# Scores of two heads in the two halves of the array, transposes as two of 64 rows, and a new order of the attention steps

## The chip, the cores and the metric

The kernel runs on one core of one Trainium2 chip. The metric is the device time of one execution in microseconds, the median of several runs. TensorE is called PE below, its weight loads PEld, VectorE DVE, ScalarE ACT, GpSimd POOL, and SyncE, which issues the large transfers, SP.

## What is computed

Two layers of a hybrid decoder over 512 tokens of width 1024. In each layer one projection makes q, k, v and a gate for 16 heads of width 64: 8 "dilated" heads, whose mask is the mixture of three dilated windows, and 8 "forgetting" heads, whose scores get a cumulative log of a forget gate as a bias. In between stands the norm of q and k, then causal softmax attention, the SiLU gate, the output projection and a gated embedding.

```python
qa = rms_norm(heads(qa), qk_g[0]); ka = rms_norm(heads(ka), qk_g[1])
s = einsum('bqhd,bkhd->bhqk', q_i, k) * scale          # forgetting heads
s = s + c_i[..., :, None] - c[:, :, None, :]           # c = cumsum(log_f)
prob = softmax(where(causal, s, NEG)); o = prob @ v
...
ob = dilated_attention(qb, kb, vb)                      # three (window, dilation) pairs
h = h + concatenate([oa * silu(ga), ob * silu(gb)]) @ w_out
gate = sigmoid(rms_norm(h, ple_norm_g) @ w_ple_gate)
h = h + (p_i @ w_ple) * gate
```

## The kernel before

All products are made exact to about fp32 by splitting each operand in a high and a low fp32r part (`hi` by ACT, `lo` by a subtraction on DVE). `mm3` (L397) is the pattern: high x high, high x low, low x high. Weights are streamed by `Weights`: SP loads them raw, `conv` splits them (L144 on ACT, L145 on DVE); `pump` asks for the next split, if a slot is free.

Heads go in pairs (`NPAIR` = 8 a layer, the first `NDIL` = 4 dilated, the others forgetting). The loop over p (L631) projects pair p, with `pj(p, t)` for each of four token tiles (24 matmuls of 384 columns, a psA bank) and `gate_mm` (24 of 512 columns), while pair a = p - 1 goes through attention:

- `att_qk` (L498) turns q and k of both heads with eight 128x128 fp32 transposes against the identity (L503) into two psM banks; ACT and DVE write QQ, KK, KL. For one head, QQ[j] holds q's high part in the 64 rows of the head and q's low part in the other 64; KK[j] holds k's high part twice; KL[j] holds k's low part and, for forgetting heads, two rows with the bias (`bias_rows`, L490, by small DMAs from ACT's queue). QA is QQ with rows of ones for the bias, copied by POOL.
- `att_s` (L529) makes the scores of one head: for each query tile one matmul QQ x KK (L541) and one with KL (L542), over all 128 rows, so that high x high and low x high are summed in one. Then, per tile: mask and row minimum on DVE (L548), exp with its sum on ACT (L550), reciprocal on DVE, scaling on POOL (L552), in place in U.
- `att_tp` (L556) turns the ten causal 128x128 blocks of one head's probabilities (L564) into three psS banks, and splits them into PT (L569, L570).
- `att_pv` (L572) makes eight matmuls (L582); its output is added up by ACT and DVE and multiplied with the gate on POOL; `att_o` (L591) splits it for the output projection.

PSUM has eight banks: psA two, psM two, psS four, each a tile of its own. The code's order is a priority: the framework schedules each engine's queue ahead of the run by that order and by which instructions it holds ready, so later work can be pulled forward. A tile of a pool is free again when its last reader is done. At the end of a layer (last p) there is no projection left, and `part(d, k0, k1)` makes the output projection as far as its inputs are there.

Of the kernel before, what the change touches and what calls it, by code (L numbers as in the profile page):

```python
# [17 lines left out]
P = 128  # L18
S = 512
# [61 lines left out]
class Weights:  # L81
    """Streams the weights: raw f32 by DMA, then split exactly into two f32r parts."""
# [24 lines left out]
    def slice_load(self):  # L107
        """first slots of the stream: loaded and split by single k slices"""
# [80 lines left out]
def trunk(tc, ap):  # L189
# [3 lines left out]
    with ctx:  # L193
# [7 lines left out]
        psM = ctx.enter_context(tc.tile_pool(name="psM", bufs=2, space=PSUM))  # L201
        psS = ctx.enter_context(tc.tile_pool(name="psS", bufs=4, space=PSUM))
        dp = ctx.enter_context(tc.tile_pool(name="dp", bufs=1, space=bass.MemoryType.DRAM))

        def ptile(pool, tag):
            return pool.tile([P, S], F32, tag=tag, name=tag)

# [46 lines left out]
        KL = [cp.tile([P, S], F32R, name=f"KL{i}") for i in range(2)]  # L254
        QA = [cp.tile([P, S], F32R, name=f"QA{i}") for i in range(2)]
# [10 lines left out]
        def rope_angles():  # L266
            """angles reduced into [-pi, pi], in steps whose products are exact"""
# [35 lines left out]
        V.memset(ones1, 1.0)  # L303
        for j in range(2):
            G.memset(KL[j].bitcast(F32), 0.0)
            G.memset(QA[j].bitcast(F32), 0.0)
            G.memset(PT[j][:, 0].bitcast(F32), 0.0)
# [3 lines left out]
        G.memset(QA[0][64:66].bitcast(F32), 1.0)  # L311
        G.memset(QA[1][0:2].bitcast(F32), 1.0)

# [61 lines left out]
        def finish_stats(pool, tag):  # L375
            """-> r (rms reciprocal) and E = eps * (mean + eps), by token; Rh = r / 2, replicated"""
# [112 lines left out]

        def bias_rows(a):  # L490
            for j, row in ((0, 64), (1, 0)):
                h = 2 * (a - NDIL) + j
                for i in range(2):
                    A.dma_start(KL[j][row + i:row + i + 1].bitcast(F32),
                                C2[32 * i + h:32 * i + h + 1].bitcast(F32))

# [1 line left out]
        def att_qk(l, a, z):  # L498
# [375 lines left out]
```

## Time and profile before

| | |
|---|---|
| median of 3 runs | 724.83 us (724.45 to 725.20) |
| span of the profiled execution | 722.8 us |
| median above that span | 2.0 us |
| PE busy | 711.5 us, 98% |
| DVE busy | 523.7 us, 72% |
| ACT busy | 419.2 us, 58% |
| POOL busy | 244.6 us, 34% |
| mean granted clock of TensorE | 0.995 |

For the profiled execution only its span is recorded; the 2.0 us are the difference of that span and the median. Busy is the time in which at least one instruction of an engine is on record; matmuls overlap, so PE's 98% leaves room for small gaps, and the distance between two starts is the better measure of what one costs.

### The profile page before, as it was taken

Reading aid. Unit: us, or ns where it says so; the run is one execution under the profiler, and the core shown is the slowest. Engines: PE = TensorE matmul, PEld = TensorE weight load, DVE = VectorE, ACT = ScalarE, POOL = GpSimd, SP = SyncE. Lnnn points to the kernel's source line nnn. Section 1 sums busy time; section 2 is a strip of 40 time slices with the busy share of each in tenths; the row PEclk is TensorE's granted clock in tenths of the full one; section 3 lists DMA queues with packets and bytes.
Section 4 is the critical chain, followed back from the end, with each engine's and each line's share of the span. In section 5 each row is a group of like instructions: output and inputs, shape, how many; then the busy total and the mean of one; then the engine's idle time right before and its main releaser. Section 6 shows DMA issues by size and latency. Waiting matters only on the chain.

```text
span 722.8 us, 11104 instructions
## 1 busy us (share of the span) xinstructions
PE 711.5 (98%) x3848; PEld 642.1 (89%) x3848; DVE 523.7 (72%) x1254; ACT 419.2 (58%) x855; POOL 244.6 (34%) x361
## 2 busy tenths in 40 slices
PE   9989999999999999999999999999999999999997
PEld 8889999999999978887899999999999997888886
DVE  7888778877786787638738887778777778584533
ACT  8575766667574676325425856757566576562310
POOL 8645636244343530000004546443353344100000
PEclk9989999999999999999999999999999999999999
DMA  8513032120312234415333022030321304352211
GB/s 293 160 53 97 22 116 69 50 88 31 118 48 70 88 106 129 146 39 193 103 105 118 23 94 89 30 117 5 113 75 45 95 24 132 102 175 88 87 44 44
DMA packets 23943, 65.46 MB, mean 91 GB/s; under 512 B 4816, under 2 KB 6096, under 8 KB 23888
## 3 DMA queue, kind: packets, MB, share of 16 engines
q1 hardware_dynamic: 22576, 64.68, 27.9%
q8 instruction: 30, 0.49, 0.3%
q10 hardware_dynamic: 1312, 0.08, 0.1%
q14 instruction: 25, 0.20, 0.1%
HBM read 60.49 MB, written 4.19 MB: 89 GB/s over the span
## 4 chain that ended last, share of the span: by engine, by line
PE 88%; DVE 4%; ACT 4%; POOL 2%; issue 1%; POOLq 0%; ACTq 0%
PE psA L398 21%; PE psA L399 20%; PE psA L400 20%; PE psM L582 5%; PE psS L564 5%; PE psS L400 2%; PE psS L399 2%; PE psS L398 2%; PE psS L542 2%; PE psS L541 2%; PE psM L503 2%; POOL f L421 1%; DVE wlo L145 1%; PE psM L398 1%; PE psM L399 1%
## 5 line engine op out<-in xcount | busy, mean ns | idle before, releaser
L144 ACT ACTIVATE whi<-raw 128x1024 fp32r<-128x1024 f32 (+3 forms) x105 | 106.9, 1023 | 96.5 <-PE psA L399 73.9
L145 DVE TENSOR_TENSOR wlo<-raw,whi 128x1024 fp32r<-128x1024 f32 (+4 forms) x103 | 120.9, 1186 | 14.6 <-ACT whi L144 14.5
L421 POOL TENSOR_TENSOR f<-ms,mhalf 128x4 f32<-128x4 f32 x64 | 78.9, 1233 | 105.2 <-DVE ms L419 101.6
L550 ACT ACTIVATE U<-U,mx 128x512 f32<-128x512 f32 (+3 forms) x128 | 70.6, 553 | 28.8 <-DVE mx L548 28.7
L398 PE MATMUL psA<-whi,X 128*128 128x384 f32 (+1 forms) x240 | 83.9, 350 | 0.0
L398 PE MATMUL psA<-whi,Y 128*128 128x384 f32 (+1 forms) x240 | 83.0, 346 | 0.0
L399 PE MATMUL psA<-wlo,X 128*128 128x384 f32 (+1 forms) x240 | 82.0, 341 | 0.0
L400 PE MATMUL psA<-whi,X 128*128 128x384 f32 (+1 forms) x240 | 81.7, 341 | 0.0
L399 PE MATMUL psA<-wlo,Y 128*128 128x384 f32 (+1 forms) x240 | 81.0, 338 | 0.0
L400 PE MATMUL psA<-whi,Y 128*128 128x384 f32 (+1 forms) x240 | 81.0, 338 | 0.0
L552 POOL TENSOR_SCALAR U<-U,sm 128x512 f32<-128x512 f32 (+3 forms) x128 | 66.0, 533 | 22.8 <-PE psS L542 9.2
L398 PE MATMUL psA<-Y,whi 128*128 128x512 f32 (+1 forms) x176 | 68.1, 387 | 0.5 <-DVE sqh L771 0.5
L399 PE MATMUL psA<-Y,whi 128*128 128x512 f32 (+1 forms) x176 | 67.8, 385 | 0.0
L400 PE MATMUL psA<-Y,wlo 128*128 128x512 f32 (+1 forms) x176 | 67.6, 384 | 0.0
L398 PE MATMUL psA<-X,whi 128*128 128x512 f32 x168 | 66.6, 397 | 0.0
L399 PE MATMUL psA<-X,whi 128*128 128x512 f32 x168 | 66.5, 396 | 0.0
L400 PE MATMUL psA<-X,wlo 128*128 128x512 f32 x168 | 66.2, 394 | 0.0
L385 POOL TENSOR_TENSOR r<-m,mhalf 128x4 f32<-128x4 f32 x4 | 4.7, 1184 | 173.6 <-DVE m L384 169.8
L589 POOL TENSOR_TENSOR U<-U,U 64x512 f32<-64x512 f32 x28 | 36.2, 1293 | 73.7 <-DVE U L587 73.7
L548 DVE CUSTOM_DVE_ANT_0 U<-psS,cst 128x512 f32<-128x512 f32 (+3 forms) x128 | 59.3, 478 | 0.2
L570 DVE TENSOR_TENSOR PT<-psS,PT 128x384 fp32r<-128x384 f32 (+1 forms) x96 | 53.0, 592 | 0.9 <-ACT PT L569 0.9
L434 DVE TENSOR_TENSOR z<-psA,f 128x256 f32<-128x256 f32 x60 | 25.5, 425 | 38.0 <-POOL f L421 38.0
(192 smaller groups left out, 1685.8 us busy)
## 6 DMA issues: line engine op xcount, KB each, us to landing
raw<-in_wq_dram SPq DMA_DIRECT2D x28, 576.0 KB, 4.0
raw<-in_wg_dram SPq DMA_DIRECT2D x16, 512.0 KB, 3.3
raw<-in_wo_dram SPq DMA_DIRECT2D x16, 512.0 KB, 3.4
raw<-in_wpg_dram SPq DMA_DIRECT2D x16, 512.0 KB, 4.1
raw<-in_wq_dram SPq DMA_DIRECT2D x14, 384.0 KB, 3.2
U<-in_xT_dram SPq DMA_DIRECT2D x16, 256.0 KB, 3.1
raw<-in_wple_dram SPq DMA_DIRECT2D x4, 512.0 KB, 4.3
hs<-U SPq DMA_DIRECT2D x8, 256.0 KB, 3.1
```

The source lines that it names most:

```text
L144: self.nc.scalar.activation(hi, r, AF.Copy)
L145: eng.tensor_tensor(lo, r, hi.bitcast(F32), op=ALU.subtract)
L398: T.matmul(out, lh, rh_, start=first, stop=False)
L399: T.matmul(out, lh, rl, start=False, stop=False)
L400: T.matmul(out, ll, rh_, start=False, stop=last)
L421: G.tensor_tensor(f, ms, mhalf.to_broadcast([P, 4]), op=ALU.pow)
L548: V.tensor_tensor_reduce(seg, tiles[qt][:, :n], mask[:, S - n:], 1.0, 3e38, ALU.add, ALU.min, mx)
L550: A.activation(seg, seg, AF.Exp, bias=mx, scale=-1.0, accum_out=sm)
L552: G.tensor_scalar(seg, seg, sm, 1.0, op0=ALU.mult, op1=ALU.mult)
L564: T.transpose(dst, pseg(j, qt)[:, kt * P:(kt + 1) * P], ident)
L570: V.tensor_tensor(lo, src, hi.bitcast(F32), op=ALU.subtract)
L589: E.tensor_tensor(U[7][b], U[7][b], U[5 + a % 2][b], op=ALU.mult)
```

## The change

- PSUM: psM becomes one buffer and psS two, each of two banks (`wide`). psA stays.
- `att_z` turns q and k with `flip`: each 128x128 block as two transposes of 64 rows, whose outputs of 64 columns go to the two banks of a wide tile. `att_qk` then splits q and k for both heads together: two copies on ACT, three subtractions on DVE. KL, QA and the copies into the other half are gone; QQ and KK are now the high and low parts, with head j in the 64 rows of half j.
- `att_s` handles both heads. Each term is one matmul of 64 rows for head 0 and one for head 1, alternating, into different banks: high x high, high x low, low x high, and for forgetting heads ones x CB, which holds the bias rows.
- `att_tp` turns both heads at once: two whole blocks and eight halved ones of each head. `att_pt` splits a head's blocks in two ACT and two DVE instructions (256 and 1024 columns).
- Order: the probabilities of pair p - 1 are turned at the end of step p, right ahead of q and k of pair p; their split and P V (`att_pv`) come in step p + 1, behind the rest of the gate's matmuls. `cumulate` is called right ahead of `bias_rows`, for p = 5. At the end of the layer the parts of the output projection are spread anew.
- Docstrings and comments are dropped.

```diff
-        psM = ctx.enter_context(tc.tile_pool(name="psM", bufs=2, space=PSUM))
-        psS = ctx.enter_context(tc.tile_pool(name="psS", bufs=4, space=PSUM))
+        psM = ctx.enter_context(tc.tile_pool(name="psM", bufs=1, space=PSUM))
+        psS = ctx.enter_context(tc.tile_pool(name="psS", bufs=2, space=PSUM))
...
+        def wide(pool, tag):
+            return pool.tile([P, 2, S], F32, tag=tag, name=tag)
...
+        HALF = (slice(0, 64), slice(64, P))
+
+        def flip(dst, src):
+            for h in range(2):
+                T.transpose(dst[:, h], src[HALF[h]], ident[HALF[h], HALF[h]])
+
+        def att_z(z):
+
+            ps = wide(psM, "psM")
+            for t in range(NT):
+                for c in (0, 2):
+                    o = (c // 2 * NT + t) * 64
+                    flip(ps[:, :, o:o + 64], z[t][:, c:c + 2].rearrange("p h d -> p (h d)"))
+            return ps
+
+        def att_qk(l, a, ps):
             kinds = (2, 3) if a < NDIL else (0, 1)
...
+            g = gq[:, l, kinds[0]:kinds[0] + 1]
+            src = ps[:, :, :256].rearrange("p h (t c) -> p h t c", t=NT)
+            hi, lo = (x.rearrange("p (t h c) -> p h t c", h=2, t=NT) for x in QQ)
+            A.activation(hi, src, AF.Copy, scale=g)
+            for h in range(2):
+                V.scalar_tensor_tensor(lo[:, h], src[:, h], g, hi[:, h].bitcast(F32), op0=ALU.mult,
                                        op1=ALU.subtract)
...
+            g = gq[:, l, kinds[1]:kinds[1] + 1]
+            src = ps[:, :, 256:]
+            hi, lo = (x.rearrange("p (h c) -> p h c", h=2) for x in KK)
+            A.activation(hi, src, AF.Copy, scale=g)
+            V.scalar_tensor_tensor(lo, src, g, hi.bitcast(F32), op0=ALU.mult, op1=ALU.subtract)
...
+        def att_s(a):
+            fox = a >= NDIL
...
+            banks = [wide(psS, "psS") for _ in range(2)]
+            pm = wide(psM, "psM")
...
+                for j in range(2):
+                    tiles[(j, qt)] = (pm[:, j, 256:], pm[:, j, :256], banks[j][:, 1, :384],
+                                      banks[j][:, 0])[qt]
+                for i, (x, y) in enumerate(((0, 0), (0, 1), (1, 0), (2, 2))[:4 if fox else 3]):
+                    for j in range(2):
+                        if x == 2:
+                            lhs, rhs = low[HALF[j]], CB[HALF[j], :nt * P]
+                        else:
+                            lhs = QQ[x][HALF[j], qt * P:(qt + 1) * P]
+                            rhs = keys(KK[y], j, nt)
+                        T.matmul(tiles[(j, qt)], lhs, rhs, start=i == 0, stop=i == 2 + fox)
...
+        def att_tp(b0):
+
+            banks = [wide(psS, "psS") for _ in range(2)]
+            blocks = [[pseg(j, qt)[:, kt * P:(kt + 1) * P] for kt in range(NT)
+                       for qt in range(kt, NT)] for j in range(2)]
+            for j in range(2):
+                for i in range(2):
+                    T.transpose(b0[:, (2 * j + i) * P:(2 * j + i + 1) * P], blocks[j][i], ident)
+            for j in range(2):
+                for i in range(8):
+                    flip(banks[j][:, :, i * 64:i * 64 + 64], blocks[j][i + 2])
...
+            for p in range(1, NPAIR):
+                a, b = p - 1, p - 2
...
+                if p > 1:
+                    gate_mm(l, a, u, gps, CG, NK)
+                    att_pt(tpb[0])
+                    gate_evac(a, gps)
+                    att_qk(l, a, pqk)
+                    pv = wide(psM, "psM")
+                    att_pv(b, 0, pv[:, 0])
+                    pj(p, 0, 0, 4)
+                    att_pt(tpb[1])
                     W.pump()
+                    att_pv(b, 1, pv[:, 1])
+                    pj(p, 0, 4, NK)
                     ev(p, 0)
...
+                    att_o(b, oo)
+                if p == 5:
+                    cumulate()
+                if a >= NDIL:
+                    bias_rows(a)
...
+                att_s(a)
...
+                gps = ptile(psA, "psA")
+                gate_mm(l, p, u, gps, 0, CG)
+                W.pump()
+                tpb = att_tp(ptile(psA, "psA"))
+                pqk = att_z(zt(p))
...
+            att_s(a)
+            W.pump()
+            part(1, 0, 6)
+            part(0, 6, 7)
+            W.pump()
+            part(1, 6, 7)
+            pv = wide(psM, "psM")
+            tpb = att_tp(pv[:, 0])
+            att_pt(tpb[0])
+            tail = wide(psS, "psS")
+            part(2, 0, 3, tail[:, 0])
+            att_pv(a, 0, pv[:, 1])
+            att_pt(tpb[1])
+            part(2, 3, 7, tail[:, 0])
+            att_pv(a, 1, pv[:, 0])
+            part(3, 0, 4, tail[:, 1])
+            att_o(a, oo)
```

## Rows read from the trace of the kernel before

**Rows 1.** Page, part 1: busy time of each engine, share of the span, instructions.
```profile
PE 711.5 (98%) x3848; PEld 642.1 (89%) x3848; DVE 523.7 (72%) x1254; ACT 419.2 (58%) x855; POOL 244.6 (34%) x361
```

**Rows 2.** Waits of the matmul engine: total us, times, longest us.
```profile
PE psM L503 <- DVE z L442: 2.8, 2, 1.8
...
PE psS L564 <- POOL U L552: 0.9, 3, 0.5
```

**Rows 3.** Timeline, matmul engine, 164 to 200: start, length (us), line, out<-moving,stationary.
```profile
166.03 0.34 PE L398 MATMUL psA<-whi,X 128*128 128x384 f32 x1
...
169.53 0.34 PE L400 MATMUL psA<-whi,X 128*128 128x384 f32 x1
169.70 0.40 PE L541 MATMUL psS<-KK,QQ 128*128 128x512 f32 x1
...
170.88 0.28 PE L542 MATMUL psS<-KL,QA 128*128 128x256 f32 x1
171.00 0.34 PE L398 MATMUL psA<-whi,X 128*128 128x384 f32 x1
...
177.02 1.25 PE L564 MATMUL psS<-cst,U 128*128 128x128 f32 x10
178.03 0.42 PE L398 MATMUL psA<-whi,X 128*128 128x384 f32 x1
178.29 0.34 PE L399 MATMUL psA<-wlo,X 128*128 128x384 f32 x1
...
184.19 0.39 PE L398 MATMUL psA<-X,whi 128*128 128x512 f32 x1
...
187.44 0.39 PE L400 MATMUL psA<-X,wlo 128*128 128x512 f32 x1
```

**Rows 4.** Single lines of code: ns min/median/max of PE matmuls and PEld weight loads.
```profile
L379 PE MATMUL psS<-ones,acc x16: 166/250/250, 20.5 to 380.5; 128*128 128x1 f32 x16
...
L564 PEld LDWEIGHTS psS<-cst,U x320: 138/140/145, 54.1 to 620.8; 128*128 128x128 f32 x160
L564 PE MATMUL psS<-cst,U x320: 270/273/335, 54.1 to 620.9; 128*128 128x128 f32 x160
...
L541 PEld LDWEIGHTS psS<-KK,QQ x128: 187/188/190, 46.3 to 614.1; 128*128 128x128 f32 x128
...
L482 PEld LDWEIGHTS psM<-tri,lf x8: 114/114/116, 133.0 to 486.3; 128*40 128x40 f32 x8
```

**Rows 5.** Groups by form: busy us, mean ns, idle before it.
```profile
L144 ACT ACTIVATE whi<-raw 128x1024 fp32r<-128x1024 f32 x52 | 55.2, 1066 | 63.1 <-PE psA L399 54.1 <-PE psS L399 6.3 <-DMA raw<-in_wple_dram 1.6
...
L416 ACT ACTIVATE sq<-psA 128x256 f32<-128x256 f32 x60 | 23.0, 383 | 33.9 <-PE psA L400 31.6 <-DVE ms L418 1.5
...
L509 ACT ACTIVATE QQ<-psM,gq 64x512 fp32r<-64x512 f32 x32 | 21.8, 681 | 4.0 <-PE psM L503 3.0 <-DVE QQ L512 0.5
...
L586 ACT ACTIVATE ob<-psM 64x512 f32<-64x512 f32 x32 | 19.1, 596 | 57.5 <-PE psM L582 57.5
...
L145 DVE TENSOR_TENSOR wlo<-raw,whi 128x1024 fp32r<-128x1024 f32 x51 | 61.8, 1219 | 2.4 <-ACT whi L144 2.4
...
L434 DVE TENSOR_TENSOR z<-psA,f 128x256 f32<-128x256 f32 x60 | 25.5, 425 | 38.0 <-POOL f L421 38.0
L512 DVE SCALAR_TENSOR_TENSOR QQ<-psM,gq,QQ 64x512 fp32r<-64x512 f32 x32 | 24.0, 750 | 1.5 <-ACT QQ L509 0.5
...
L456 DVE TENSOR_TENSOR U<-psA,Rh 128x512 f32<-128x512 f32 x14 | 9.7, 691 | 7.1 <-PE psA L400 7.0
```

**Rows 6.** Timeline of ACT, 163 to 196, and DMA issues of the bias rows.
```profile
171.20 0.50 ACTq L494 DMA_DIRECT2D KL<-C  x1
...
KL<-C ACTq DMA_DIRECT2D x32, 2.0 KB, 1.6
```

**Rows 7.** Windows, the last pair of each layer: length, busy us of each engine.
```profile
253.00:266.00 13.00, 12.45 (x65) 9.85 (x64) 11.68 (x35) 10.92 (x27) 6.24 (x10) 1.00 0.23 70
585.00:616.00 31.00, 30.66 (x168) 26.52 (x166) 25.26 (x76) 21.98 (x53) 14.71 (x19) 1.00 0.25 78
```

More of the change, by code (lines that the diff above doesn't have):

```diff
@@ L520, in pseg, with keys @@
+        def keys(x, j, nt):
+            return x.rearrange("p (h t c) -> p t h c", h=2, t=NT)[HALF[j], :nt]
         def pseg(j, qt):
@@ L569, in att_tp, with att_pt, att_pv @@
+        def att_pt(banks):
+            whole, half = banks
+            h2 = [x[:, 3:11].rearrange("p a (h c) -> p h a c", h=2) for x in PT]
+            w2 = [x[:, 1:3] for x in PT]
+            for src, (hi, lo) in ((whole, w2), (half, h2)):
                 A.activation(hi, src, AF.Copy)
                 V.tensor_tensor(lo, src, hi.bitcast(F32), op=ALU.subtract)
-        def att_pv(a, j):
-            ps = ptile(psM, "psM")
+        def att_pv(a, j, ps):
             v2 = V2[a % 2]
@@ L597, in trunk, with four @@
         stats0 = None
-        first = [ptile(psA, "psA") for _ in range(2)] + [ptile(psM, "psM") for _ in range(2)]
+        def four():
+            pm = wide(psM, "psM")
+            return [ptile(psA, "psA") for _ in range(2)] + [pm[:, i] for i in range(2)]
+        first = four()
         for d in range(NK):
@@ new lines, in trunk, with part, zt @@
+            dps = {}
+            def part(d, k0, k1, ps=None):
+                if k0 == 0:
+                    dps[d] = ptile(psA, "psA") if ps is None else ps
+                wh, wl = W.get(("o", l, d))
+                for k in range(k0, k1):
+                    mm3(dps[d], wh[:, k, :], wl[:, k, :], oo[0][:, k], oo[1][:, k], k == 0,
+                        k == NK - 1)
+                if k1 == NK:
+                    W.done(("o", l, d))
+            def zt(p):
+                return [zs[(p, t)] for t in range(NT)]
@@ new lines, in trunk @@
+            if l > 0:
+                first = four()
+                for t in range(NT):
+                    proj(l, 0, t, u, first[t], 0, NK - 1)
+                stats0 = finish_stats(psS, "psS")
+                for t in range(NT):
+                    proj(l, 0, t, u, first[t], NK - 1, NK)
+            st["r"], st["E"], rh = stats0
+            W.pump(PA)
+            W.pump(PB)
+            for t in range(NT):
+                cur[t] = first[t]
+                ev(0, t)
+                if t == 1:
+                    W.pump(PC)
@@ new lines, in trunk @@
+            a, b = NPAIR - 1, NPAIR - 2
+            gate_mm(l, a, u, gps, CG, NK)
+            att_pt(tpb[0])
+            gate_evac(a, gps)
+            att_qk(l, a, pqk)
+            bias_rows(a)
+            pv = wide(psM, "psM")
+            att_pv(b, 0, pv[:, 0])
+            W.pump()
+            part(0, 0, 3)
+            att_pt(tpb[1])
+            W.pump()
+            att_pv(b, 1, pv[:, 1])
+            part(0, 3, 6)
+            att_o(b, oo)
+            att_s(a)
+            W.pump()
@@ L748, in trunk @@
             for d in range(NK):
-                part(d, 7 if d < 3 else 0, NK, (psA, psS)[d % 3 == 2])
+                if d == 5:
+                    tail = wide(psS, "psS")
+                part(d, 7 if d < 3 else 4 if d == 3 else 0, NK, tail[:, 0] if d == 5 else None)
                 V.tensor_tensor(U[d], U[d], dps[d], op=ALU.add)
```

220 lines of the change are left out of this document (53 added, 167 removed).

## The prediction

> **What bounds the kernel now.** I read the engine shares first: the matmul engine is busy for 711.5 of 722.8 us, every other engine for at most 72% [rows 1]. Busy time can hide gaps, since one matmul's record overlaps the next, so I looked at its waits next: transposes of q and k wait 2.8 us in the whole run, those of probabilities 0.9 [rows 2]. Last the timeline of one pair, for the distance from start to start, which is what a matmul really costs [rows 3]: 20 steps from 166.03 to 169.53 give 0.175 us for 384 columns, 14 steps from 184.19 to 187.44 give 0.232 for 512, and 256 columns take 0.12. The scores of one head, eight matmuls, run from 169.70 to 171.00, 1.30 us. Ten transposes run from 177.02 to 178.03, and the matmul behind them comes 0.26 instead of 0.175 before its successor, so they cost 1.095 us, 0.109 each. A pair's 96 projection and 24 gate matmuls, its scores, P V and 28 transposes follow each other at these distances with nothing between: time is won only by taking work from the matmul engine, and lost wherever it is made to wait. The median of the runs, 724.83, is 2.0 us above the profiled span; sums below are made on the span and carried over by that difference.
>
> **Scores.** Before, a head needs two matmuls per query tile over 128 rows: 2 x 1.30 = 2.60 us per pair. Afterwards each product uses 64 rows, three terms for a dilated pair and four for a forgetting pair (the bias becomes a term of its own), and the two heads stand in different halves of the array. If the halves run at once, one term over the four query tiles costs half of 1.30, so three cost 1.95 and four 2.60 [rows 3]: 0.65 us won in each of 8 dilated pairs, 5.2 us; nothing in the forgetting pairs. If they take turns it is 3.90 and 5.20. No matmul of the trace uses half of the rows, so both are bounds.
>
> **Transposes.** 28 blocks per pair cost 28 x 0.109 = 3.05 us. What limits one? A matmul of one column takes at least 166 ns, a transpose of 128 fp32 columns 270, so streaming takes 104 ns of the 109; its weight load is recorded with 140 ns against 188 for the fp32r loads [rows 4]. A load of 40 columns takes 114 and of 128 takes 188, so 0.84 ns per column with 80 fixed; that leaves 60 ns for the transpose's load and 108 for an fp32r load [rows 4]. So the stream of the identity is the limit, and two halves of 64 columns that run at once would take half, 0.055 us. Afterwards 4 blocks stay whole and 24 are halved: 4 x 0.109 + 24 x 0.055 = 1.76, 1.29 us won per pair, 20.6 in 16 pairs. The other bound is two loads in turn, 2 x 60 = 119 ns per block: 3.30 per pair, 0.25 lost. I take the halves at once, for both kinds, because a load of 60 ns already hides under a stream of 104 in the same array [rows 4]. Together 5.2 + 20.6 = 25.8 us won.
>
> **What the new order costs.** The wide psM is one buffer of two banks: q and k turned, then both outputs, then the small scores. So P V of pair b can't start before att_qk has read the turned q and k. Take zero at the first transpose. The whole blocks end at 0.44, the first head's halves at 0.88, the second's and those of q and k at 1.76, the gate's last nine matmuls (9 x 0.232) at 3.85. The chain beside it, with some 0.05 us at each hand-over: ScalarE copies 1024 columns of the first head (1.07), VectorE subtracts them (1.22) [rows 5], which ends at 3.27; then the two halves of q's low part (two at about 0.43) and k's (0.75) [rows 5] end at 4.9. ScalarE's two copies of q and k (0.68 each) lie beside it. The other bank that PE could use is the gate's; its 0.69 us multiply [rows 5] is queued on VectorE between those, and comes to 4.9 too. So PE has nothing from 3.85 to 4.9: 1.05 to 1.1 us. I count 1.1 for 7 pairs of each layer: 14 x 1.1 = 15.4 us given back. Behind the wait stand P V and the projection's first tile, thus the whole pair. The bounds are 0, if the scheduler finds VectorE free sooner, and 2.3, where a weight split (1.22) is queued in between: 0 to 32 us.
>
> The second head's PT copy must wait for the first's P V: ob 0.60, copies 0.38 + 1.07, subtract 1.22 [rows 5], 3.3 us with hand-overs; 24 projection matmuls (24 x 0.175 = 4.2) cover it if they are pulled forward, which I take, as the order in the trace isn't the program's: the bias DMAs of the next pair are issued at 171.20, right behind the last score matmul that reads KL at 170.88, although the code has them an iteration later [rows 3, 6]. Without that cover it costs about 1.2 us a pair, inside the bound above. bias_rows moves behind att_o on ScalarE's queue, four DMAs with 0.5 us of issue and 1.6 to landing [rows 6]; being issued early, they cost nothing. For the first forgetting pair they hang on cumulate, now directly ahead: some 5.3 us of small copies and the landing, against 4.2 us of the next projection tile; I take 0, bound 1.1 to 5.3 per layer.
>
> At the end of a layer nothing stands behind the last transposes: part 2 needs a psS pair that att_pt is still reading, psA holds parts 0 and 1. PE waits from 1.32 to about 3.3, 1.9 us, and 0.6 more for the second head (3.4 against 12 x 0.232 = 2.8). The old tail lost 0.55 and 0.34 us [rows 7]. Net 2 x 2.5 - 0.9 = 4 us.
>
> Each pair now changes between full and half rows four times, where it had three groups of transposes. The 0.085 us seen behind a group [rows 3] is the nearest row: 16 more of them, 1.4 us. The upper bound is the 166 ns that a lone matmul needs from end to end [rows 4], 64 times: 10.6 us. I take the lower, since the row shows a change of operand type with no more than that. The Trainium skill ("TensorEngine Tiling (Array Packing)", Tiling Modes) says that changing the tiling mode drains the engine; no run here shows a change of mode. By it the term would be 10.6, the second rival below.
>
> ScalarE loses four copies of about 0.65 us per pair and VectorE one subtraction in effect; both were covered by PE, so this is worth nothing by itself, and its cover isn't needed. The POOL copies of q go for the same reason.
>
> **Sum.** 722.8 - 25.8 + 15.4 + 4 + 1.4 = 717.8 of span, 719.8 in the median: 720.
>
> **Rivals.**
> First, the waits are filled: VectorE is free early and the tail is no worse than before. Then 724.8 - 25.8 + 1.4 + about 1 = 701. For it: PE waited almost nowhere so far [rows 2]. Against: the chain above is 1 us longer than its cover by rows alone. Chance 0.16.
>
> Second, the array empties at each change of rows: 10.6 in place of 1.4, 729. Decides if a change costs above 0.11 us more than I took. Chance 0.12.
>
> Third, the other side: the halves stream together but their weight loads go one behind the other. Then a pair of score matmuls costs 2 x 0.108 = 0.215 us whatever its width: 12 of them 2.58 (nothing won), 16 of them 3.44 (0.84 lost, 8 times, 6.7 us); transposes lose 16 x 0.25 = 3.9. With slower transposes the gate's tail ends later and PE waits about 0.6 us, 14 times, 8. Sum 724.8 + 6.7 + 3.9 + 8 + 4 + 1.4 = 749. It decides once a 64-row load in turn takes above some 85 ns. For it: every full load takes its 108 ns, and no two matmuls of the trace start nearer than 0.10 us. Chance 0.20. The Trainium skill ("TensorE: Matmul & The Clock Gate", LDWEIGHTS) says that a load's time goes by its columns, not its rows; the 40-column row agrees on columns, and no row here shows fewer rows. By that rule a half's load is as long as a whole one, which is this rival's price.
>
> Fourth, nothing runs side by side, so the change doesn't do what it says: scores lose 8 x 1.30 + 8 x 2.60 = 31.2; 724.8 + 31.2 + 3.9 + 8 + 4 + 1.4 = 773. Chance 0.10.
>
> **How the numbers follow.** My forecast, 720, has 0.42; its own range, from a wait of 0.6 to 1.7 us a pair, is 713 to 728. Below and above are 0.16 at 701, 0.12 at 729, 0.20 at 749 and 0.10 at 773. About 0.2% is what a measurement of this kernel can tell from no change, so same means 723.4 to 726.3. Faster: 0.32 of my own case, all of the first rival, 0.02 of the second, 0.50. Same: 0.06 and 0.01, 0.07. Slower: the rest, 0.43. The range runs from 700, which takes in the first rival, to 752, which takes in the third and leaves out the fourth and the edges.
>
> **What would show it.** In the trace afterwards: the two halves of a score term start together and the next term 0.23 us later for 512 columns (mine) or 0.46 (fourth); 16 halved transposes of a head take 0.44 us (mine) or 0.95 and more (third). Between the gate's last matmul and the next work PE should idle 1.1 us, ended by VectorE's low part of k or by the gate's multiply; if it idles for under 0.3, the first rival holds. The gap at the first matmul behind each group shows the change of rows: 0.09 or 0.17 us. I am wrong if the wait stands elsewhere, above all before the scores (small scores waiting for P V's bank) or at the first forgetting pair's bias.

## The result and the profile after

The changed kernel takes 780.48 us (779.99 to 781.59) against 724.71 of the kernel before on the same chip: a ratio of 1.0769, with a 95% interval of 1.0754 to 1.0784. The forecast was 720 us, with a range from 700 to 752: wrong in its sign, and far outside the range.

The page's first part and its chain of work that ended last, which answer to [rows 1]:

```profile
PE 724.4 (93%) x4424; PEld 626.6 (80%) x4424; DVE 506.4 (65%) x1204; ACT 382.6 (49%) x759; POOL 231.8 (30%) x340
...
PE 48%; DVE 17%; ACT 13%; issue 12%; POOL 9%; DMA 0%; ACTq 0%; POOLq 0%; DVEq 0%
```

The same chain of the kernel before:

```profile
PE 88%; DVE 4%; ACT 4%; POOL 2%; issue 1%; POOLq 0%; ACTq 0%
```

Every other engine has less to do than before, and yet PE alone is no longer what sets the end: VectorE, ScalarE and GpSimd hold 39% of the chain where they held 10%, so PE now waits for them. The waits of the matmul engine, in total us, times and longest us, which answer to [rows 2]:

```profile
PE psA L400 <- DVE z L436: 15.8, 12, 1.7
PE psA L586 <- DVE z L436: 11.3, 10, 1.9
PE psS L565 <- ACT KK L529: 7.1, 12, 0.6
PE psA L400 <- DVE sqh L816: 3.3, 3, 1.4
PE psM L565 <- DVE c L488: 3.0, 2, 1.5
...
PE psA L400 <- DVE U L458: 0.5, 2, 0.4
```

The wait on which the forecast rested, for the gate's multiply (the last line), hardly occurs; at its place, behind the gate's last matmul, PE waits for k's high part instead (third line). The first two are new, the third had 0.7 us before, and each stands in 10 to 12 of the 16 pairs. The timeline of the matmul engine, one dilated pair (start, length, line, out<-moving,stationary), which answers to [rows 3]:

```profile
110.73 1.31 PE L565 MATMUL psS<-KK,QQ 64*128 64x512 f32 x10
...
112.85 0.44 PE L400 MATMUL psA<-whi,X 128*128 128x384 f32 x1
113.14 0.34 PE L401 MATMUL psA<-wlo,X 128*128 128x384 f32 x1
...
121.19 0.34 PE L402 MATMUL psA<-whi,X 128*128 128x384 f32 x1
123.24 0.41 PE L400 MATMUL psA<-whi,X 128*128 128x384 f32 x1 [1.71 <-DVE z L436]
...
130.79 0.40 PE L402 MATMUL psA<-X,wlo 128*128 128x512 f32 x1
132.05 0.63 PE L586 MATMUL psA<-cst,U 128*128 128x128 f32 x4 [0.86 <-DVE z L436]
132.61 1.22 PE L506 MATMUL psS<-cst,U 64*128 64x64 f32 x32
133.66 0.66 PE L506 MATMUL psM<-cst,z 64*128 64x64 f32 x16
134.26 0.50 PE L400 MATMUL psA<-X,whi 128*128 128x512 f32 x1
134.59 0.39 PE L401 MATMUL psA<-X,whi 128*128 128x512 f32 x1
...
136.21 0.39 PE L402 MATMUL psA<-X,wlo 128*128 128x512 f32 x1
137.20 0.50 PE L565 MATMUL psS<-KK,QQ 64*128 64x512 f32 x1 [0.60 <-ACT KK L529]
137.63 0.44 PE L400 MATMUL psA<-whi,X 128*128 128x384 f32 x1
137.91 0.34 PE L401 MATMUL psA<-wlo,X 128*128 128x384 f32 x1
```

What the change was to win is there: 23 of a pair's 24 score matmuls take 112.85 - 110.73 = 2.1 us, where two heads took 2.6; 32 halved transposes take 133.66 - 132.61 = 1.05 us, 0.066 a block against 0.109 [rows 3]. Where PE stands still: 2.05 us ahead of the fourth projection tile (121.19 to 123.24, where 0.175 is usual), 1.26 us ahead of the whole blocks (130.79 to 132.05, where 0.23 is usual), and 0.99 us (136.21 to 137.20, where 0.23 is usual) ahead of one score matmul that the schedule pulled forward. And the change of rows shows: behind 64-row work a full matmul comes 0.28 or 0.33 us before its successor where 0.175 and 0.23 are usual.

The first of these waits, followed back. A projection tile needs one of two psA banks, and the bank is free when z is made from it: square on ACT (L418), row sums on DVE, power on POOL, z on DVE (L436). ACT and DVE around it:

```profile
115.94 0.73 ACT L574 ACTIVATE U<-U,mx 128x512 f32<-128x512 f32 x1 [2.22 <-DVE mx L572]
...
119.94 0.39 ACT L574 ACTIVATE U<-U,mx 128x128 f32<-128x128 f32 x1
...
120.33 0.36 ACT L418 ACTIVATE sq<-psA 128x256 f32<-128x256 f32 x1
...
134.37 0.69 ACT L522 ACTIVATE QQ<-psM,gq 128x512 fp32r<-128x512 f32 x1
136.46 0.69 ACT L529 ACTIVATE KK<-psM,gq 128x512 fp32r<-128x512 f32 x1 [1.41 <-DVE QQ L524]
```

```profile
122.67 0.42 DVE L436 TENSOR_TENSOR z<-psA,f 128x256 f32<-128x256 f32 x1 [1.14 <-POOL f L423]
...
135.56 0.87 DVE L524 SCALAR_TENSOR_TENSOR QQ<-psM,gq,QQ 128x256 fp32r<-128x256 f32 x2
```

The second tile's 24 matmuls start at 112.85, the last of them at 116.99, so they end at some 117.3. Its square starts at 120.33, behind eight exps of both heads that run from 115.94 to 120.3 in one block; z follows at 122.67 and the matmul at 123.24.

To add all this up, take for every matmul the distance from its start to the next one's, and take off the usual distance of its own kind. For all columns of the table this is the median of the full matmuls, 0.232 us for 512 columns, 0.174 for 384, 0.118 for 256 and 0.109 for a whole transpose; for 64 rows it is half of these, and 0.033 for a halved transpose. In us (in brackets how often):

| | before | after | e6 | e14 | e15 | e11 |
|---|---|---|---|---|---|---|
| all matmuls at their medians | 698.8 | 677.0 | 677.0 | 677.1 | 688.1 | 687.8 |
| excess from 64 rows to 64 rows | - | 6.4 | 4.4 | 1.6 | 1.4 | -0.2 |
| excess at changes of rows | - | 14.7 (98) | 13.2 (107) | 11.0 (93) | 8.1 (67) | 7.1 (66) |
| excess from full to full | 11.5 | 17.2 | 15.6 | 15.0 | 16.6 | 13.5 |
| waits above 0.4 us | 6.2 (7) | 58.2 (51) | 35.0 (35) | 32.4 (36) | 26.2 (30) | 9.4 (10) |
| first to last matmul | 716.5 | 773.5 | 745.1 | 737.1 | 740.4 | 717.7 |

The change wins 21.8 us of PE work, pays 21.1 of it back beside the halved matmuls and at changes of rows and 5.7 from full to full, and 52 us of new waits make the result. These are sums over the profiled executions; that of the changed kernel, 781.59 us, is the slowest of its four, so the table has 57.0 us where the medians have 55.8.

Most of the 5.7 belongs to the changes of rows too. The first full matmul behind 64-row work comes 0.106 us too late before its successor (56 times, 6.5 us in all). Before, the first one behind a group of whole transposes came 0.085 too late (58 times), but there the last transpose stood 0.081 us nearer to it than usual, so that a group cost next to nothing. The experiments (e6 and so on) follow.

### The profile page after: what moved, and what is told of

The parts are those of the page before. It is cut to its first block, busy times and chain, and to the rows that moved or that the text cites. A ratio compares the mean times of both kernels' runs of the same rounds, so it can differ in the third digit from the quotient of the medians.

```text
span 779.8 us, 12097 instructions
## 1 busy us (share of the span) xinstructions
PE 724.4 (93%) x4424; PEld 626.6 (80%) x4424; DVE 506.4 (65%) x1204; ACT 382.6 (49%) x759; POOL 231.8 (30%) x340
## 4 chain that ended last, share of the span: by engine, by line
PE 48%; DVE 17%; ACT 13%; issue 12%; POOL 9%; DMA 0%; ACTq 0%; POOLq 0%; DVEq 0%
PE psA L400 11%; PE psA L402 10%; PE psA L401 10%; ACT U L574 7%; POOL f L423 6%; PE psM L610 5%; DVE z L436 2%; DVE PT L599 2%; DVE wlo L145 2%; DVE ms L421 2%; ACT PT L598 2%; PE psS L565 2%; PE psS L506 1%; DVE U L572 1%; PE psS L400 1%
## 5 line engine op out<-in xcount | busy, mean ns | idle before, releaser
L423 POOL TENSOR_TENSOR f<-ms,mhalf 128x4 f32<-128x4 f32 x64 | 73.4, 1146 | 85.8 <-DVE ms L421 81.8
L400 PE MATMUL psA<-Y,whi 128*128 128x512 f32 (+1 forms) x168 | 66.0, 394 | 2.7 <-DVE sqh L816 1.9
L400 PE MATMUL psA<-X,whi 128*128 128x512 f32 x160 | 64.3, 403 | 2.8 <-DVE sqh L816 1.4
L401 PE MATMUL psA<-Y,whi 128*128 128x512 f32 (+1 forms) x168 | 64.8, 386 | 0.0
L402 PE MATMUL psA<-Y,wlo 128*128 128x512 f32 (+1 forms) x168 | 64.6, 385 | 0.0
L401 PE MATMUL psA<-X,whi 128*128 128x512 f32 x160 | 63.3, 396 | 0.0
L402 PE MATMUL psA<-X,wlo 128*128 128x512 f32 x160 | 63.1, 394 | 0.0
L436 DVE TENSOR_TENSOR z<-psA,f 128x256 f32<-128x256 f32 x60 | 25.3, 422 | 56.6 <-POOL f L423 56.6
L400 PEld LDWEIGHTS psA<-whi,X 128*128 128x128 f32 x240 | 45.8, 191 | 11.8 <-issue 7.7
L400 PEld LDWEIGHTS psA<-whi,Y 128*128 128x128 f32 x240 | 45.1, 188 | 11.7 <-issue 7.4
```

What stands on the lines that cost most here:

```text
L400: T.matmul(out, lh, rh_, start=first, stop=False)
L401: T.matmul(out, lh, rl, start=False, stop=False)
L402: T.matmul(out, ll, rh_, start=False, stop=last)
L423: G.tensor_tensor(f, ms, mhalf.to_broadcast([P, 4]), op=ALU.pow)
L436: V.tensor_tensor(z, ps[:, :2 * P].rearrange("p (h d) -> p h d", h=4), f[:, :, None].to_broadcast([P, 4, HD]), op=ALU.mult)
```

## The experiments

All times below stand against the kernel before on the same chip, 724.4 to 725.2 us. W is the theory that PE waits for buffers at the places seen above; H, that these are only the visible end of something else.

**The three waits, one by one.** e1_kk_first makes the high part of k ahead of the subtractions for q, since the copy at 136.46 waited for one of them:

```diff
             A.activation(hi, src, AF.Copy, scale=g)
+            A.activation(khi, srck, AF.Copy, scale=gk)
             for h in range(2):
                 V.scalar_tensor_tensor(lo[:, h], ...)
-            A.activation(khi, srck, AF.Copy, scale=gk)
```

> Edit: in att_qk ScalarE copies q's and k's high parts one after the other, ahead of VectorE's subtractions. Theory W (the time is lost in waits that the new order of steps and buffers makes, the halves themselves run side by side): in the changed kernel the first score matmul of a step waits 0.75 us for k's high part, 12 times, 9 us; the copy stands behind VectorE's work on q in the same PSUM bank. So 772 to 777. Rival H (the halves and the changes between full and half rows cost the time; a wait that is taken away comes back at the next place): 779 to 782.

Measured: 775.78 us, 1.0699 [1.0681, 1.0717], 4.7 less than the changed kernel: W. That the wait for k's high part is gone shows in e4, which has this edit: none is left there.

e2_softmax_by_head puts the second head's softmax behind the next projection tile in the code:

```diff
-                att_s(a)
+                soft = att_s(a)
+                soft(0)
                 pj(p, 1)
                 ev(p, 1)
+                soft(1)
```

> Edit: the softmax is issued by head, and the second head's stands behind the next projection tile and its evacuation. Theory W: the fourth projection tile waits 1.1 to 1.9 us for a psA buffer, whose evacuation is queued behind eight exps on ScalarE, about 10 times, 17 us; it goes for the most part: 764 to 770. Rival H: 778 to 782.

Measured: 781.79 us, 1.0784 [1.0766, 1.0802], no gain. It looks like H, but the edit did not reach the chip's queue: its waits for z ahead of projection tiles are still 12 in number, 17.4 us in sum, and ACT still has the eight exps in one block. The order of the code is a priority, and the scheduler took the exps when they were ready. The test was left to e5.

e3_whole_last turns the whole blocks, which want a psA bank, behind the halved ones, which want psS, and splits them in that order:

```diff
+            for j in range(2):
+                for i in range(8):
+                    flip(banks[j][:, :, i * 64:i * 64 + 64], blocks[j][i + 2])
             for j in range(2):
                 for i in range(2):
                     T.transpose(b0[...], blocks[j][i], ident)
-            for j in range(2):
-                for i in range(8):
-                    flip(banks[j][:, :, i * 64:i * 64 + 64], blocks[j][i + 2])
...
-            for src, (hi, lo) in ((whole, w2), (half, h2)):
+            for src, (hi, lo) in ((half, h2), (whole, w2)):
```

> Edit: the four whole transposes stand behind the halved ones, and att_pt splits the halved blocks first. Theory W: the whole ones wait 1.0 to 2.1 us for a psA buffer that the last projection tile still holds, 12 times, 15 us; 32 halved transposes of 1.06 us now stand ahead of them: 766 to 770. Rival H: 778 to 782.

Measured: 769.65 us, 1.0619 [1.0603, 1.0634], 10.8 less: W. The wait for that bank falls from 11.3 us to 1.7:

```profile
PE psA L589 <- DVE z L436: 1.7, 3, 0.8
```

The 10.8 us are not this wait alone: the wait for KK falls as well, from 7.1 to 2.6 us, that for z ahead of projection tiles rises from 15.8 to 17.5, and rows change 120 times instead of 98.

e4_three_mended joins them.

> Edit: the edits of e1, e2 and e3 together. Theory W: the three waits are 9, 17 and 15 us, and most of them goes, if nothing else is late: 740 to 752. Rival H: above 770.

Measured: 766.00 us, 1.0567 [1.0549, 1.0584], between the two. It is the sum of e1 and e3 alone, 780.5 - 4.7 - 10.8 = 765.0; the softmax still stands as before.

**The softmax, with a dependence.** e5_sq_ahead gives ACT no choice:

```diff
+                with tc.issue_after(st["sq"].ins):
                     soft(1)
```

> As the kernel with the three mended waits (766.0 us), and the exps of the second head now wait, by a dependence on ACT, for the square of projection tile 1. Theory W: the fourth projection tile waits 1.7 us, 15 times, because that square stands behind eight exps of both heads on ACT; the dependence takes that wait away, up to 15 us of the 17 recorded, so 749 to 756. Rival H: that wait is only the visible end of a longer chain on DVE and POOL (the square's row sums, the power, z), so moving the square alone shifts nothing: above 762.

Measured: 754.00 us, 1.0402 [1.0387, 1.0418], 12.0 less than e4: W. ACT now has four exps, the square, four exps, and the wait for z ahead of the fourth projection tile is gone (2 waits, 1.0 us left of 12, 15.8). Two lines of e5's waits:

```profile
PE psA L400 <- DVE U L458: 5.1, 14, 0.5
...
PE psA L400 <- DVE z L436: 1.0, 2, 0.7
```

So a fifth of the loss (12.0 of 55.8) hung, with e1 and e3 in place, on one small ScalarE instruction behind eight exps.

**What is left.** e6_scores_not_pulled makes the score matmuls depend on the last P V matmul of the pair before:

```diff
-                    att_pv(b, 1, pv[:, 1])
+                    pvl = att_pv(b, 1, pv[:, 1])
...
-                soft = att_s(a)
+                soft = att_s(a, pvl if p > 1 else None)
```

> As the run before, and the score matmuls come only behind the last P V matmul of the pair before, so that no single score matmul of 64 rows stands between the projection's full matmuls. Theory W: the lone matmul costs a change into half rows and back and 0.74 us of a wait behind it, 14 times, so 7 to 11 us less than e5_sq_ahead (740 to 748). Rival H: the wait is that of the gate's bank, which stays whatever stands ahead of it: within 3 us of e5_sq_ahead.

Measured: 753.55 us, 1.0403 [1.0386, 1.0421], nothing against e5: H. The wait has only got another place: what PE no longer waits around the score matmul, it waits for the gate's multiply (L458), 5.1 us in e5 and 11.1 here. One line of e6's waits, then its matmul timeline:

```profile
PE psA L400 <- DVE U L458: 11.1, 14, 0.9
```

```profile
127.97 0.39 PE L402 MATMUL psA<-X,wlo 128*128 128x512 f32 x1
129.26 0.44 PE L400 MATMUL psA<-whi,X 128*128 128x384 f32 x1 [0.90 <-DVE U L458]
```

This is the wait of the forecast, at last: 14 times, for the gate's multiply (L458). Here it is 129.26 - 127.97 = 1.29 less the usual 0.23, 1.06 us; the other 13 are 0.94 or 0.95, against 1.1 forecast. In the changed kernel the pulled score matmul and its wait for KK stood in its place.

e7_more_gate_behind tries to cover it with more of the gate's matmuls behind the transposes:

```diff
-C2S, C3A, C3B, CG = 5, 1, 7, 5
+C2S, C3A, C3B, CG = 5, 1, 7, 3
```

> As the run before, with three instead of five of the gate's eight k steps ahead of the transposes, so that 15 instead of 9 gate matmuls (1.39 us more) stand behind them while q, k and the probabilities are split. Theory W: what is left of the wait ahead of P V and of the projection's first tile is under 1.4 us a pair and is covered: 5 to 12 us less than e6_scores_not_pulled. Rival H: the transposes come 1.39 us sooner and now wait for the last projection tile's z and the bank it holds: within 3 us of it or slower.

Measured: 756.91 us, 1.0445 [1.0429, 1.0462], slower: H. The gate's wait is gone, and the transposes, 1.4 us sooner, wait 16.1 us in all (13 times) for the bank of the last projection tile. By the same sums as in the table the waits stay as they are, 34.6 us against 35.0 in e6.

e9_gate_whole goes the other way: all of the gate and its multiply ahead of the transposes, the whole blocks first among these again.

```diff
-                gate_mm(l, p, u, gps, 0, CG)
+                gate_mm(l, p, u, gps, 0, NK)
+                gate_evac(p, gps)
                 W.pump()
                 tpb = att_tp(ptile(psA, "psA"))
```

> As e6_scores_not_pulled, but all 24 gate matmuls and the gate's multiply stand ahead of the transposes (and the two whole blocks first among these again, so that rows change once less a pair). What is left to wait in e6 is 14 times 0.95 us for the gate's multiply, which is queued on DVE behind the splits of the probabilities and of q, and 6 times 0.8 us for the bank of the whole blocks. Theory W: the first is gone, as the multiply now runs beside the transposes and the next projection tile can follow them at once; the second is covered by the nine gate matmuls that come first (2.1 us); 0.29 us less for a change of rows, 14 times: 753.5 - 13 - 5 - 4 = 731, between 728 and 737. Rival H: PE then waits for P V instead, as the splits of the probabilities (two copies and subtractions, 3 us and more) have only one projection tile beside them: above 745.

Measured: 768.79 us, 1.0611 [1.0595, 1.0627]: H, by more than I thought. Its waits:

```profile
PE psA L400 <- DVE sm L580: 9.1, 10, 1.5
PE psM L617 <- DVE KK L530: 7.2, 14, 1.3
PE psM L570 <- DVE U L622: 4.5, 10, 0.6
```

Gone is the wait for the gate's multiply; come are P V behind k's low part in psM (second line), the small scores behind P V's readers in the same psM (third), and projection tiles behind the softmax again (first).

e10_cumulate_apart is e9 with the cumulated gate logs one pair earlier and in psA:

```diff
-            ps = ptile(psM, "psM")
+            ps = ptile(psA, "psA")
...
-                if p == 5:
+                if p == 4:
                     cumulate()
```

> As e9_gate_whole, with the cumulated gate logs one pair earlier and in a psA bank in place of the wide psM. Theory W: the wait of the small scores at the first forgetting pair (1.1 to 1.5 us in either layer) is for the bank, not for the bias rows, and goes: 2 to 3 us less than e9. Rival: another projection tile waits for the psA bank then: no change.

Measured: 762.89 us, 1.0523 [1.0502, 1.0544], 5.9 less than e9, twice what I expected. The wait meant by W is gone: by the same sums as in the table 1.7 us of small scores behind the cumulated logs (L488), and 2.0 us more that cumulate's own matmuls waited for psM. But other waits take their place, 49.9 us in all in e9 and 49.4 here. The gain comes from fewer changes of rows (82 to 70, 1.7 us) and less slack between 64-row matmuls (2.4) and full ones (1.6). So W holds for the wait and does not explain the gain. The releaser in the trace of the changed kernel, L488, is the last reader of that psM bank, so it was the bank that the small scores waited for; the run by itself does not tell it from the earlier bias rows.

e14_bank_freed_early is e6 with that edit, and with the second head's whole blocks split into SBUF of their own (PW), so that their psA bank is free before the gate ends:

```diff
+                    att_pw(tpb[1])
                     gate_evac(a, gps)
                     att_qk(l, a, pqk)
```

> As e6_scores_not_pulled, with two blocks of SBUF more: the whole blocks of the second head are split ahead of P V of the first head, so that their psA bank is free before the gate's last matmuls end (P V of the second head makes its first product in two matmuls of 256 columns). The cumulated logs are in a psA bank one pair earlier. Theory W, PE waits because all eight banks are taken: the 14 waits of 0.95 us for the gate's multiply go, and the two of 1.2 us for cumulate's bank: 753.5 - 13.2 - 2.4 = 738, between 735 and 743. Rival H: another bank or engine is next late within some tenths of a us, as in e9_gate_whole: above 747.

Measured: 745.37 us, 1.0287 [1.0269, 1.0305], between W and H. Its waits:

```profile
PE psA L401 <- DVE sm L581: 5.3, 6, 1.1
PE psM L571 <- DVE U L635: 4.4, 12, 0.7
PE psA L596 <- DVE z L437: 4.3, 6, 0.8
```

None of the 14 waits for the gate's multiply is left, and at their place PE waits once, 0.5 us, for the split into PW, so a free bank was what lacked. But PE gets to the small scores sooner, and these now wait, 12 times, for psM, which P V's readers still hold (second line, 4.4 us), and projection tiles wait behind the softmax for 5.3 us (first line) where e6 has 1.3. These two are about what the gain falls short by: 8 us where 15.5 were expected. It is the best kernel with the new order, and still 20 us slower than before.

**The halves.** e8_halves_in_turn is the changed kernel with the two loops that alternate between the halves turned round:

```diff
-                for i, (x, y) in enumerate(...):
-                    for j in range(2):
+                for j in range(2):
+                    for i, (x, y) in enumerate(...):
...
-                for i in range(8):
-                    flip(banks[j][...], blocks[j][i + 2])
+                for h in range(2):
+                    for i in range(8):
+                        T.transpose(banks[j][:, h, ...], blocks[j][i + 2][HALF[h]], ...)
```

> The changed kernel with one difference: score matmuls and halved transposes of one half of the rows all come first, then those of the other half, so that neighbours never stand in different halves. If the halves run side by side (my reading of the trace): a dilated pair's scores take 3.9 instead of 2.1 us, a forgetting pair's 5.2 instead of 2.8, and 48 halved transposes twice 33 ns or more each, 1.6 us or more a pair: 8 x 1.8 + 8 x 2.4 + 16 x 1.6 = 59 us at most, less what the longer PE work covers of the waits: 805 to 840. If nothing runs side by side and the halves only are cheap by themselves: 778 to 785.

Measured: 781.30 us, 1.0783 [1.0767, 1.0799]. By the expectation this would speak for "nothing side by side", but the trace says why it doesn't:

```profile
108.33 1.31 PE L565 MATMUL psS<-KK,QQ 64*128 64x512 f32 x10
...
110.46 0.44 PE L400 MATMUL psA<-whi,X 128*128 128x384 f32 x1
```

The scores take the same 2.13 us, and their matmuls start in pairs again, although three of one half now stand ahead of three of the other in the queue. PE had taken the other half's matmuls out of turn: at 108.90 a matmul of 384 columns starts 0.01 us ahead of one of 512 columns of the other half that stands before it in the queue. The run did not separate the theories; greater distance should.

e13_halves_far_apart puts 12 or 16 score matmuls of one head ahead of the other's, and 16 and 8 halved transposes of one half ahead of the other's:

```diff
-            for qt in (3, 2, 1, 0):
-                ...
-                    for j in range(2):
+            for j in range(2):
+                for qt in (3, 2, 1, 0):
...
+            for h in range(2):
                 for j in range(2):
                     for i in range(8):
```

> The changed kernel, with all score matmuls of one head (12 or 16) ahead of those of the other, and all halved transposes of one half of the rows (16, then 8) ahead of those of the other half. If halves run side by side only where matmuls of both stand near each other in the queue, they now run one by one: a dilated pair's scores 3.5 to 3.9 us instead of 2.1, a forgetting pair's 4.7 to 5.2 instead of 2.8, and 48 halved transposes 0.062 us each (as the first five in e8_halves_in_turn) instead of 0.033: 8 x 1.6 + 8 x 2.1 + 16 x 1.4 = 52 us more, of which the waits behind may hide a third: 810 to 835. If nothing ran side by side in the changed kernel: 778 to 785.

Measured: 795.97 us, 1.0979 [1.0963, 1.0996], 15.5 more than the changed kernel.

```profile
113.77 1.26 PE L567 MATMUL psS<-KK,QQ 64*128 64x512 f32 x5
...
117.24 0.44 PE L400 MATMUL psA<-whi,X 128*128 128x384 f32 x1
...
135.05 1.84 PE L592 MATMUL psS<-cst,U 64*128 64x64 f32 x29
...
137.62 0.50 PE L400 MATMUL psA<-X,whi 128*128 128x512 f32 x1
```

The scores take 3.47 us where they took 2.1, the 48 halved transposes 2.57 where they took 1.65: the halves of the changed kernel do run side by side. By the same sums the excess from 64 rows to 64 rows grows from 6.4 to 44.3 us, 38 more. The time grows by 15.5 alone, as the waits shrink from 58.2 us to 35.4: more than half of this PE work fell into waits that were there anyway. That is why the expectation was too high, and it holds the other way round: work taken from PE here is won only in part.

e12_blocks_whole undoes one part, halving the probabilities' blocks, in e10:

```diff
-                    flip(banks[j][:, :, i * 64:i * 64 + 64], blocks[j][i + 2])
+                    T.transpose(banks[j][:, i // 4, ...], blocks[j][i + 2], ident)
```

> As e10_cumulate_apart, but one part of the change undone: the probabilities' other eight blocks of a head are turned whole too, those of q and k stay halved. 256 blocks by 0.109 - 0.066 us: if that is what halving is worth with the order mended, 11 us more than e10, between 8 and 13. If PE still waits behind the transposes for what reads them, a part of it vanishes in these waits: under 6 us more.

Measured: 761.79 us, 1.0514 [1.0497, 1.0532]: not slower than e10 but 1.1 less, inside the intervals. Halving the blocks was worth nothing there: by the same sums as in the table PE has 11.0 us more work, but 9.0 less waits and 2.7 less slack between full matmuls.

e15_bank_early_whole does the same to e14.

> As e14_bank_freed_early, with the probabilities' other eight blocks of a head turned whole, 0.69 us a pair more work for PE (16 x 0.043). If PE is again the limit there: 8 to 11 us more than e14. If it still waits behind the transposes for what reads them: within 5 us of e14.

Measured: 748.44 us, 1.0323 [1.0306, 1.0340], 3.1 more than e14, so PE still waits there. By the table 11.0 us more at the medians, but 2.9 less at changes of rows (26 fewer) and 6.2 less in waits: the longer transposes cover the wait for the whole blocks' bank.

e11_halved_alone is that one part in the kernel before, in the old order, where PE hardly waits (6.2 us in the table):

```diff
+            for i in range(8):
+                for h in range(2):
+                    r = slice(64 * h, 64 * h + 64)
+                    T.transpose(banks[1 + h][:, i * 64:i * 64 + 64], blocks[i + 2][r], ident[r, r])
```

> The kernel before, with one part of the change alone: eight of the ten probability blocks of a head are turned as two of 64 rows into a pair of psS banks, in the old order, head by head. 256 blocks by 0.109 - 0.066 us are 11.0 us won; rows change twice for each of 32 heads. At the prices of the trace after (0.10 us into 64 rows, 0.19 out) that costs 9.3 us: 723, between 721 and 726. At the prices of my forecast (0.055 us for a block, 0.085 for a change) it would be 724.8 - 13.8 + 5.4 = 716. If halving a block won nothing by itself: 734.

Measured: 726.44 us, 1.0026 [1.0016, 1.0036], a little slower than before and just outside the 721 to 726 expected.

```profile
177.22 0.38 PE L561 MATMUL psS<-cst,U 128*128 128x128 f32 x2
177.53 0.71 PE L565 MATMUL psS<-cst,U 64*128 64x64 f32 x16
178.17 0.44 PE L398 MATMUL psA<-whi,X 128*128 128x384 f32 x1
178.45 0.34 PE L399 MATMUL psA<-wlo,X 128*128 128x384 f32 x1
```

The second whole block starts 0.11 us behind the first, so 0.20 before the halves: 0.09 for the change. Eight halved blocks end 0.64 later, 0.11 more than 16 by 0.033, and the next matmul stands 0.10 too long. The table gives the sum: 11.0 us won at the medians, 7.1 lost at 66 changes of rows, 3.2 in waits and 2.0 from full to full, 1.2 more in all from first to last matmul. Even in the old order this part buys nothing: it wins 0.34 us a group, pays some 0.28 of it (7.1 and 2.0 us over 33 groups) for going into 64 rows and back, and the waits take the rest. The expectation had these costs at 9.3 us, near the 9.1, and no waits.

## Why the prediction was wrong

**That the halves run side by side** was right: 2.1 us for a pair's scores (1.95 forecast), 0.033 us a halved transpose in a run of both halves (0.0275 forecast: 0.44 us for 16, found 0.53). The rivals that loads go in turn and that nothing runs side by side fall with e13. 25.8 us were to be won; at the medians it is 21.8, and 6.4 go in slack between halved matmuls. On the loads: a 64-row load is on record with 147 to 186 ns in the mean, a full one with 140 (transposes) or 188 [rows 4], but those of the two halves mostly start within some 10 ns of each other. So a load's time does not go by its rows, and the rival built on it still failed, since the loads overlap. One reading that spoke for that rival was wrong: in the trace before, 58 matmuls start 0.026 to 0.031 us behind another, each the first one behind a group of transposes, and not 0.10 or more.

**The change of rows** was mis-sized: 1.4 us forecast with 10.6 as upper bound, 14.7 found. A change costs 0.10 us into 64 rows (46 times, 4.8 us) and 0.19 out of them (52 times, 9.9), 0.15 in the mean, near the bound of 0.166 that I did not take; and there are 98 of them that can be read apart from waits, not 64, as the schedule pulls single score matmuls between full ones. With the 6.5 us at the first full matmul behind 64-row work it is 21 us. I had taken a change of operand type as the nearest row for a change of rows, and even that row was no price: the 0.085 us behind a group of transposes makes up for a last transpose that stands 0.081 us nearer than usual, and it is already in the 0.109 us a block, which were worked out with it. The Trainium skill ("TensorEngine Tiling (Array Packing)", Tiling Modes) says that a change of tiling mode drains the array; the trace agrees as far as each change costs time, 0.10 to 0.19 us. By that sentence my second rival, 729, was the better base.

**The waits** were the failing step: 15.4 us at one place, between the gate's last matmul and P V, and 4 at the tails, where the table has 52 us. At that one place PE does idle, 12 times (9.0 us in the sums of the table), but for k's high part, which a pulled score matmul wants, and twice for the gate's multiply (1.3). With the score matmul held back, e6 shows the forecast wait itself, 14 times some 0.95 us. The tails have 6.2 us of waits against 1.0 before, near my 4. What I had put at nothing makes the difference: 17.7 us ahead of projection tiles and 13.1 ahead of the whole blocks, both for a psA bank. Smaller, and put at nothing as well, are 3.3 us at the first forgetting pair and 3.2 in the gated embedding (two waits of 1.6 us, the line with L816), which no version with the new order took away and whose cause was not tested.

What I did not ask is what the new order does in the rest of the pair. Before, scores, transposes and P V of the heads stood between projection tiles and gave psA's banks time to come free. Afterwards the scores of both heads stand together at the front, three projection tiles follow in a row with two banks, and just then ACT and DVE have the softmax of both heads in one block. I had counted ACT's and DVE's load as covered by PE, which holds for their shares of busy time, but the fourth projection tile waits for a 0.36 us square that stands behind that block. By the times of the runs this one wait is worth 12.0 us (e4 to e5), the order that mends the wait for the whole blocks' bank 10.8 (e3), the copy of k 4.7 (e1).

**The scheduler.** I took it that the second head's copy would be covered because projection would be pulled forward. It was pulled forward, but so were score matmuls, one by one, which cost two changes of rows each and a wait for KK. Holding them back (e6) gained nothing, as the next wait stood behind them.

**The first forgetting pair** I took at 0 with a bound of 1.1 to 5.3 us a layer. It waits 1.5 us in either layer (L488 in the waits above), by its releaser for psM and not for the bias rows; in e10, which moves it, it is gone, though the 5.9 us gained there are mostly something else. The tails were not tested apart.

**The rivals.** The one on the slower side was wrong in its mechanism, and the time lies even above the last rival, 773. No rival said that PE would stop being the bound in the middle of a pair. The sum by the steps, in us from first to last matmul: -21.8 + 6.4 + 14.7 + 5.7 (full to full) + 52.0 = 57.0, against -25.8 + 1.4 + 19.4 = -5.0 forecast.

**What stays open.** In e14 32 us of waits and 11 us of changes of rows are left. They are spread over psA behind the softmax, psM behind P V and the whole blocks' bank; behind each mended wait so far another stood. Whether an order exists in which all three are covered was not found. The small scores in other banks, and a shorter way from square to z, were not tried. No run separates the new order from the wide PSUM tiles, so how much of the waits either makes is not shown. No version beat the kernel before.

## What to carry to other kernels

Where PE has 98%, an order that groups the attention work of two heads takes away the very work that gave PSUM banks time to come free: walk through a whole pair, bank by bank, and ask for each tile when its last reader is queued, not only where the new step stands. A wide PSUM tile with one buffer makes its users wait for each other, as the small scores for P V's readers in e14; that two narrow ones would have kept them apart was not run. And a halved transpose saves only 0.043 us a block, so a group needs six or seven blocks (0.28 us in e11) before it has paid for its two changes of rows.

## What the runs showed of the hardware

- Matmuls of 64 rows in the two halves run side by side with no help from the order of the queue, if they stand near each other: with three of one half ahead of three of the other (e8) the scores still take 2.13 us, and matmuls of the two halves start out of their order in the queue. With eight ahead of eight the overlap is partial (in e8 the 48 halved transposes of that pair, 32 of them in such groups, take 2.06 us against 1.65 in the changed kernel and 2.57 in e13). With 12 to 16 (e13) they run one behind the other but for the edge.
- A change between full and 64 rows costs 0.10 us one way and 0.19 back in the changed kernel, 0.09 and 0.12 in e11 (3.1 us at 33 changes, 4.0 at 33). The way back costs 0.12 behind transposes and 0.15 behind scores in the median, and 0.31 behind a single score matmul, of which 0.12 is that it runs alone and is charged as one of two; the first full matmul after it takes 0.106 us too long on top.
- A 64-row fp32 transpose takes 0.062 us when its half runs alone (the median distance in e13) and 0.033 when both run, against 0.109 for a whole block.
